# Sliding-window attention of a decoder layer: both key tiles folded into one block of 128 probabilities

## The chip, the cores and the metric

The kernel runs on one NeuronCore of a Trainium2 chip. Its engines work side by side, each on a queue of its own: TensorE (PE, with its weight loads as PEld), VectorE (DVE), ScalarE (ACT), GpSimd (POOL) and SyncE (SP, which issues most DMAs). The metric is the device time of one execution in microseconds. TensorE writes to PSUM, of which there are 8 banks of 128 x 512 float32; VectorE and ScalarE read them.

## The reference

One decoder layer for x of 1024 x 1024, float32. A norm and one projection feed two groups of heads: gated linear attention (4 heads), computed in chunks, and sliding-window attention (8 query heads, 2 key heads of 64, window 128). Then an output projection and a gated feed-forward part of width 2816 with a causal convolution of 3 taps. The change touches the sliding-window part, in which a query block of 128 rows sees its own key block and the one before:

```
i = arange(128)[:, None];  j = arange(256)[None, :]
dist = 128 + i - j
mask = (dist >= 0) & (dist < 128) & (key_abs >= 0)
s = where(mask, q k^T / 8 - slope * dist, -inf)
m = max(max(s, -1), sink)
p = exp(s - m);  p = p / (sum(p, -1) + exp(sink - m))
o = p v
```

Of the 256 keys that a row is scored against, exactly 128 lie in the window: key column c of the earlier block (j = c) where c > i, and of the own block (j = 128 + c) where c <= i. For each column c one of the two is in and the other out. The first query block has no earlier one.

## The kernel before

Rows are cut into 8 tiles t of 128. Up to some 75 us the norm and the query projection run, from then to 280 us the other projections (`dk`, `dv`, `dg`, `dr`: dense units of 24 matmuls, three for each of 8 blocks of the contraction) with both kinds of attention between them, then the output projection (`do`) and from some 370 us the feed-forward part (`fb`, `dn_P`), which no line of the change touches.

For each t, and each of two groups g of four heads, the attention steps are:

- `swa_qt(t)`: four transposes of the queries into a bank (`qpt`), split by ScalarE and VectorE into a high part `qt` and a rest `ql`.
- `swa_scores(t, g)`: eight matmuls of 256 columns put four heads' scores into two banks (`sc`). For each head VectorE adds a table `dist` (the distance, -1e30 outside the window), takes the maximum with the sink and writes the row of 256 to `pr` (line 451). Small VectorE operations make the scaled negative maximum (`sm1`). ScalarE takes the exponential of each head's 256 columns and their sum (line 457). The sums and the sink give a reciprocal (`sm2`, `sm3`, lines 459 to 462), and GpSimd multiplies all of `pr` by it (line 464).
- `swa_pt(t, g)`: for each of the two key blocks b, four transposes (`ppt`) into a bank; ScalarE copies the bank of the own block (b = 1) to `pt`, VectorE that of the earlier one (b = 0).
- `swa_pv(t)`: matmuls of the values with both halves of `pt` into a bank `pv`, which ScalarE copies out.

For t = 0 only the own block is worked on. Banks come from `bank(name)`, which takes them in turn from two pools of four. `qt`, `ql`, `pr` and `pt` are tiles of one ring of six (`k4`), smaller temporaries of a ring of four (`k2`).

The program is written as a list of events with due times (`at(s + 3.2, swa_pt, t, 0)` and so on, in units of about one dense unit), issued in the order of these times. Behind it a scheduler sets the order of each engine's queue from a model of the instructions' lengths, so that an edit moves neighbours too. The linear attention needs a mask of its own, `amask` (line 115), which `const_b` makes from an upper triangle of ones, `upper` (lines 140 to 150).

Of the kernel before, what the change touches and what calls it, by code (L numbers as in the profile page):

```python
# [9 lines left out]
F32 = mybir.dt.float32  # L10
F32R = mybir.dt.float32r
I32 = mybir.dt.int32
AF = mybir.ActivationFunctionType
ALU = mybir.AluOpType
# [3 lines left out]
P = 128  # L18
# [16 lines left out]
def hymba_layer_kernel(ctx, tc, x, mix_norm, w_in, w_alpha2, b_alpha, gla_norm,  # L35
# [3 lines left out]
    act, dve, pool, pe, sp = nc.scalar, nc.vector, nc.gpsimd, nc.tensor, nc.sync  # L39
# [15 lines left out]
    def bank(name):  # L55
        ps["n"] += 1
        if "f" in ps:
            return ps["f"][2 + ps["n"] % 2]

        for start, which in (("n2pt_6", "b"), ("do1_7", "a"), ("n2pt_3", "a")):  # L60
            if name.startswith(start):
                return ps[which].tile([P, 512], F32, tag="b", name=name)
        return ps["ab"[ps["n"] % 2]].tile([P, 512], F32, tag="b", name=name)
# [3 lines left out]
    RAW_BUFS, K4, K2, N_WARM = 3, 6, 4, 5  # L67
# [30 lines left out]
    ident = idp.tile([P, P], F32, name="ident")  # L98
# [5 lines left out]
    gl = sg.enter_context(tc.tile_pool(name="gl", bufs=1))  # L104
# [7 lines left out]
    islope = gl.tile([P, 8], F32, name="islope")  # L112
    qscale = gl.tile([P, 8], F32, name="qscale")
    tri = gl.tile([P, 2, P], F32R, name="tri")
    amask = gl.tile([P, P], I32, name="amask")
    ind = gl.tile([P, 2], F32R, name="ind")
    mhalf = idp.tile([P, 8], F32, name="mhalf")
    pool.memset(mhalf, -0.5)
# [18 lines left out]
                           fill=NEG, base=-1, channel_multiplier=-1)  # L137

    def const_b():
        upper = gl.tile([P, 512], F32, tag="k2", name="upper", bufs=K2)[:, 0:P]  # L140
        pool.memset(upper, 1.0)
        pool.affine_select(out=upper, in_=upper, pattern=[[1, P]], compare_op=ALU.is_ge,
                           fill=0.0, base=0, channel_multiplier=-1)
        pool.memset(ind.bitcast(F32), 0.0)
        pool.memset(ind[0:64, 0:1].bitcast(F32), 1.0 / 16.0)
        pool.memset(ind[:, 1:2].bitcast(F32), 1.0 / 16.0)

        dve.tensor_scalar(tri[:, 0], upper, 1.0 / 16.0, ind[:, 0:1].bitcast(F32), op0=ALU.mult, op1=ALU.subtract)
        dve.tensor_scalar(tri[:, 1], upper, -1.0 / 16.0, 1.0 / 16.0, op0=ALU.mult, op1=ALU.add)
        pool.tensor_copy(amask, upper)  # L150


    xts = {}
# [119 lines left out]
    def k4_tile(name, dt=F32):  # L273
        return gl.tile([P, 1024], dt, tag="k4", name=name, bufs=K4)
# [160 lines left out]
    def swa_scores(t, g):  # L435
        q, ql = qts[t]
        s0 = P if t == 0 else 0
        pbs = []
        for j in range(4):
            if j % 2 == 0:  # L440
                pbs.append(bank(f"sc{t}_{g}_{j}").rearrange("p (j s) -> p j s", j=2))
            qc, kc = slice(j * P, (j + 1) * P), slice(t * P, t * P + 256)
            pe.matmul(pbs[-1][:, j % 2, :], lhsT=q[:, g, qc], rhs=kt[:, g, kc], start=True, stop=False)  # L443
            pe.matmul(pbs[-1][:, j % 2, :], lhsT=ql[:, g, qc], rhs=kt[:, g, kc], start=False, stop=True)
        if g == 0:
            smx[t] = [gl.tile([P, 8], F32, tag=f"sm{i}", name=f"sm{i}_{t}", bufs=2) for i in range(4)]
        mx, nm, den, es = smx[t]
        pr = k4_tile(f"pr{t}_{g}").rearrange("p (j s) -> p j s", j=4)
        for j in range(4):
            h = g * 4 + j  # L450
            dve.tensor_tensor_reduce(pr[:, j, s0:], pbs[j // 2][:, j % 2, s0:], dist[:, s0:], 1.0,
                                     sinks_s[:, h:h + 1], ALU.add, ALU.max, mx[:, h:h + 1])
        hs = slice(g * 4, g * 4 + 4)
        dve.tensor_mul(nm[:, hs], mx[:, hs], slope_n[:, hs])
        for j in range(4):
            h = g * 4 + j
            act.activation(pr[:, j, s0:], pr[:, j, s0:], AF.Exp, bias=nm[:, h:h + 1],
                           scale=2.0 ** -(h + 1), accum_out=den[:, h:h + 1])
        dve.tensor_add(es[:, hs], sinkb[:, hs], nm[:, hs])
        act.activation(es[:, hs], es[:, hs], AF.Exp)  # L460
        dve.tensor_add(den[:, hs], den[:, hs], es[:, hs])
        dve.reciprocal(den[:, hs], den[:, hs])  # L462
        n = 256 - s0
        pool.tensor_tensor(pr[:, :, s0:], pr[:, :, s0:],  # L464
                           den[:, hs].rearrange("p (j o) -> p j o", o=1).broadcast_to((P, 4, n)),
                           ALU.mult)
        pts[t, g] = pr

    def swa_pt(t, g):
        pr = pts[t, g]  # L470
        pt = k4_tile(f"pt{t}_{g}").rearrange("p (b c) -> p b c", b=2)
        for b in range(1 if t == 0 else 0, 2):
            pb = bank(f"ppt{t}_{g}_{b}")
            for j in range(4):
                pe.transpose(pb[:, j * P:(j + 1) * P], pr[:, j, b * P:(b + 1) * P], ident)  # L475
            if b:
                act.copy(pt[:, b], pb)
            else:
                dve.tensor_copy(pt[:, b], pb)
        pts[t, g] = pt  # L480

    def swa_pv(t):
# [587 lines left out]
    for c in halves:  # L1070
        split(mix_row[:, c], mix_hl[0][0:1, c], mix_hl[1][0:1, c], dve)
        pb = bank(f"mix{len(mix_ps)}")
# [25 lines left out]
    for t in range(NT):  # L1098
# [19 lines left out]
        if 4 <= t < 7:  # L1118
            at(u + SUMS, norm2_sums, t)
    at(5.3, const_a)  # L1120
    at(TV + 1.5, const_b)
    for i in range(4):
        d = 0.2 * i
# [10 lines left out]
    for t in range(NT):  # L1134
        s = 11.0 + 1.9 * t
        at(s - 0.3, swa_qt, t)
        at(s + 1.0, swa_scores, t, 0)
        at(s + 1.6, swa_scores, t, 1)
        at(s + 3.2, swa_pt, t, 0)
        at(s + 3.8, swa_pt, t, 1)  # L1140
        at(s + 4.9, swa_pv, t)
        s = TG + t
        at(s - 2.4, gla_lh, t)
        at(s - 1.4, gla_exp, t)
        at(s + 1.0, gla_tr, t)
        if t < NT - 1:
            at(s + 1.8, gla_state, t)
            at(s + 1.85, gla_mid, t + 1)
        at(s + 1.9, gla_a, t)
        at(s + 2.7, gla_o, t)  # L1150
        at(TR + t + 1.3, lambda tt=t: gate_tr(tt, psb.pop(("r", tt))))
# [37 lines left out]
    for ch, i, name in order:  # L1189
# [7 lines left out]
        if ch < 2 or (ch, i) == (2, 0):  # L1197
            n = 0
        elif ch < L - 1 or (ch, i) == (L - 1, 0):
            n = 1  # L1200
        else:
            n = 2
# [24 lines left out]
    for p in range(NPAIR):  # L1227
        for k in range(7):

            n = 7 * p + k - 2  # L1230
# [51 lines left out]
```

## Time and profile before

| what | us |
|---|---|
| median of 3 runs | 1065.81 (1065.1 to 1065.97) |
| profiled execution | 1065.66 |
| its span, first to last instruction | 1063.9 |
| TensorE busy | 1057.7 (99%) |
| VectorE busy | 788.4 (74%) |
| GpSimd busy | 629.1 (59%) |
| ScalarE busy | 495.2 (47%) |

Busy time counts an engine's instructions from start to end, and matmuls overlap, so that a full TensorE row does not say how much a matmul costs; the chain of waits, which follows the work that ended last, gives each piece the time until the next one. The granted TensorE clock is at its upper level (2.4 GHz, 1.00) in the whole span.

### The profile page before, as it was taken

How to read it: one execution, taken by the hardware profiler on the slowest of the kernel's cores; microseconds unless marked ns; L12 is line 12 of the kernel's file. 1: busy time of each engine (PE TensorE's matmuls, PEld its weight loads, DVE VectorE, ACT ScalarE, POOL GpSimd, SP SyncE). 2: the span in 40 equal slices, each digit the busy share in tenths (PEclk: the TensorE clock that was granted, in tenths of full speed). 3: DMA queues.
4: the chain of work that ended last, by engine and by line, in shares of the span. 5: the costliest groups of instructions: out<-in, count | busy, mean ns of one | idle time of the engine just before them, and what ended most of it. 6: DMA issues, size and time to landing. Idle time of an engine off the chain costs nothing.

```text
span 1063.9 us, 13937 instructions
## 1 busy us (share of the span) xinstructions
PE 1057.7 (99%) x4988; PEld 857.0 (81%) x4988; DVE 788.4 (74%) x1306; ACT 495.2 (47%) x1002; POOL 629.1 (59%) x511
## 2 busy tenths in 40 slices
PE   9999999999999999999999999999999999999998
PEld 6898878877888888788888888888888888888887
DVE  6776546564132499787989889797979898897976
ACT  5527655544340245545444444454444445444441
POOL 4582323334551104867868787877868687868750
PEclk9999999999999999999999999999999999999999
DMA  6152123102026202112111111112121111212104
GB/s 214 57 155 56 43 53 84 24 1 80 1 60 217 60 1 60 60 40 80 39 51 49 41 59 60 60 40 79 40 79 31 51 54 45 60 60 60 41 20 158
DMA packets 67502, 67.13 MB, mean 63 GB/s; under 512 B 4648, under 2 KB 52201, under 8 KB 67434
## 3 DMA queue, kind: packets, MB, share of 16 engines
q1 hardware_dynamic: 63448, 61.27, 18.7%
q10 hardware_dynamic: 3986, 4.99, 2.0%
q8 instruction: 39, 0.64, 0.3%
q14 instruction: 29, 0.24, 0.1%
HBM read 57.33 MB, written 4.19 MB: 58 GB/s over the span
## 4 chain that ended last, share of the span: by engine, by line
PE 99%; DMA 1%; POOL 0%; SPq 0%; ACT 0%; DVE 0%; issue 0%
PE fb L815 39%; PE dn_P L996 18%; PE do L318 8%; PE dg L318 4%; PE dr L318 4%; PE dv L318 4%; PE dq L318 3%; PE dk L318 2%; PE gb L815 2%; PE dq L688 2%; PE pv L487 2%; PE ppt L475 1%; PE dl L1025 1%; PE fb L1025 1%; PE sc L443 1%; PE go L582 1%
## 5 line engine op out<-in xcount | busy, mean ns | idle before, releaser
L1000 DVE TENSOR_TENSOR acc<-acc,dn_P 128x1024 f32<-128x1024 f32 x140 | 169.8, 1214 | 65.3 <-PE dn_P L996 65.1
L996 PE MATMUL dn_P<-dw,dg 128*128 128x512 f32 x840 | 215.8, 393 | 0.0
L996 PEld LDWEIGHTS dn_P<-dw,dg 128*128 128x128 f32 x840 | 157.7, 188 | 37.1
L318 PE MATMUL do<-wow,big 128*128 128x512 f32 x384 | 92.9, 398 | 0.0
L95 POOL TENSOR_TENSOR dw<-dn,dw 128x512 fp32r<-128x512 f32 x50 | 69.5, 1390 | 25.4 <-PE dn_P L996 22.3
L318 PEld LDWEIGHTS do<-wow,big 128*128 128x128 f32 x384 | 71.1, 188 | 16.3
L867 ACT COPY ca<-fb 128x512 f32<-128x512 f32 x62 | 36.4, 587 | 72.5 <-PE fb L815 72.4
L464 POOL TENSOR_TENSOR pr<-pr,sm 128x1024 f32<-128x1024 f32 (+1 forms) x16 | 28.6, 1789 | 65.4 <-DVE sm L462 40.1
L815 PE MATMUL fb<-big,A11w 128*128 128x512 f32 x252 | 63.0, 396 | 0.0
L815 PE MATMUL fb<-big,S4w 128*128 128x512 f32 x252 | 62.9, 396 | 0.0
L815 PE MATMUL fb<-big,S1w 128*128 128x512 f32 x252 | 62.9, 396 | 0.0
L815 PE MATMUL fb<-ex,S2w 128*128 128x512 f32 x252 | 62.8, 397 | 0.0
L815 PE MATMUL fb<-ex,S3w 128*128 128x512 f32 x252 | 62.8, 396 | 0.0
L822 DVE SCALAR_TENSOR_TENSOR ua<-fb,cc,ua 128x511 f32<-128x511 f32 x84 | 62.2, 740 | 0.5 <-ACT ua L827 0.3
L815 PE MATMUL fb<-big,A12w 128*128 128x512 f32 x252 | 62.5, 396 | 0.0
L815 PE MATMUL fb<-ex,A22w 128*128 128x512 f32 x252 | 62.5, 397 | 0.0
L815 PEld LDWEIGHTS fb<-big,S1w 128*128 128x128 f32 x252 | 47.4, 188 | 11.6
L815 PEld LDWEIGHTS fb<-big,A11w 128*128 128x128 f32 x252 | 47.4, 188 | 11.6
L815 PEld LDWEIGHTS fb<-big,S4w 128*128 128x128 f32 x252 | 47.4, 188 | 11.6
L815 PEld LDWEIGHTS fb<-ex,S2w 128*128 128x128 f32 x252 | 47.4, 188 | 11.4
L815 PEld LDWEIGHTS fb<-ex,A22w 128*128 128x128 f32 x252 | 47.4, 188 | 11.4
L815 PEld LDWEIGHTS fb<-ex,S3w 128*128 128x128 f32 x252 | 47.4, 188 | 11.4
(430 smaller groups left out, 2450.6 us busy)
## 6 DMA issues: line engine op xcount, KB each, us to landing
up<-in_w_up_dram SPq DMA_DIRECT2D x44, 512.0 KB, 3.8
dn<-in_w_down_dram SPq DMA_DIRECT2D x22, 512.0 KB, 3.5
acc<-in_x_dram SPq DMA_DIRECT2D x8, 512.0 KB, 7.5
out_dram<-acc SPq DMA_DIRECT2D x15, 256.0 KB, 2.0
xt<-in_x_dram SPq DMA_DIRECT2D x7, 512.0 KB, 4.5
vraw<-in_w_in_dram SPq DMA_DIRECT2D x4, 512.0 KB, 3.8
graw<-in_w_in_dram SPq DMA_DIRECT2D x4, 512.0 KB, 3.7
qt<-qt ACTq DMA_DIRECT2D x16, 128.0 KB, 2.2
```

What stands on the lines that cost most here:

```text
L95: (eng or pool).tensor_sub(lo, src, hi.bitcast(F32))
L318: pe.matmul(pb[:, :n], lhsT=big[:, t, k, ra, :], rhs=ws[k][:, rb, :n], start=(k == 0 and i == 0), stop=(k == KD - 1 and i == 2))
L443: pe.matmul(pbs[-1][:, j % 2, :], lhsT=q[:, g, qc], rhs=kt[:, g, kc], start=True, stop=False)
L464: pool.tensor_tensor(pr[:, :, s0:], pr[:, :, s0:], den[:, hs].rearrange("p (j o) -> p j o", o=1).broadcast_to((P, 4, n)), ALU.mult)
L487: pe.matmul(pb[g * 64:(g + 1) * 64, :], lhsT=vv[:, t - 1 + b, g * 64:(g + 1) * 64], rhs=pts[t, g][:, b, :], start=(b == b0), stop=(b == 1))
L688: pe.matmul(pb, lhsT=big[:, t, k, ra, :], rhs=blocks["q"][k][:, rb, :], start=(k == 0 and i == 0), stop=(k == KD - 1 and i == 2))
L815: pe.matmul(pb, lhsT=w[:, ra, k, :], rhs=b_operand(bn, k, rb), start=(onto is None and i == 0), stop=(i == 11), skip_group_check=onto is n ...
L822: dve.scalar_tensor_tensor(dst, src, w, dst, op0=ALU.mult, op1=ALU.add)
L867: act.copy(dst, pb)
L996: pe.matmul(pb[:, i], lhsT=g[:, ra, c:c + P], rhs=w[:, rb, :], start=(onto is None and n == 0), stop=(n == 2), skip_group_check=onto is no ...
L1000: dve.tensor_add(acc, acc, pb)
L1025: pe.matmul(pb[:, c0:c1], lhsT=g[:, ra, (t % 4) * P:(t % 4 + 1) * P], rhs=w[:, rb, c0:c1], start=(ch == NCH - 2 and i == 0), stop=(ch == N ...
```

## The change

After the four score steps of a pair (t, g) with t > 0, VectorE takes the maximum of the two halves of `pr`; the result has 128 columns per head. Exponential, sum, normalisation and transposes work on those alone, one bank of transposes instead of two. Behind the transposes VectorE multiplies the bank by the triangle `upper` (keys of the own block) into the second half of `pt`, and subtracts that from the bank into the first half (keys of the earlier block). For t = 0 ScalarE copies the bank as before. The score matmuls, the score steps and `pv` keep their shapes. `upper` becomes a tile of its own that lives as long as `amask` did, and `amask` is the same bytes read as integers.

```diff
@@ -112,7 +112,8 @@
     islope = gl.tile([P, 8], F32, name="islope")
     qscale = gl.tile([P, 8], F32, name="qscale")
     tri = gl.tile([P, 2, P], F32R, name="tri")
-    amask = gl.tile([P, P], I32, name="amask")
+    upper = gl.tile([P, P], F32, name="upper")
+    amask = upper.bitcast(I32)
     ind = gl.tile([P, 2], F32R, name="ind")
     mhalf = idp.tile([P, 8], F32, name="mhalf")
     pool.memset(mhalf, -0.5)
@@ -137,7 +138,6 @@
                            fill=NEG, base=-1, channel_multiplier=-1)
 
     def const_b():
-        upper = gl.tile([P, 512], F32, tag="k2", name="upper", bufs=K2)[:, 0:P]
         pool.memset(upper, 1.0)
         pool.affine_select(out=upper, in_=upper, pattern=[[1, P]], compare_op=ALU.is_ge,
                            fill=0.0, base=0, channel_multiplier=-1)
@@ -147,7 +147,6 @@
 
         dve.tensor_scalar(tri[:, 0], upper, 1.0 / 16.0, ind[:, 0:1].bitcast(F32), op0=ALU.mult, op1=ALU.subtract)
         dve.tensor_scalar(tri[:, 1], upper, -1.0 / 16.0, 1.0 / 16.0, op0=ALU.mult, op1=ALU.add)
-        pool.tensor_copy(amask, upper)
 
 
     xts = {}
@@ -452,31 +451,34 @@
                                      sinks_s[:, h:h + 1], ALU.add, ALU.max, mx[:, h:h + 1])
         hs = slice(g * 4, g * 4 + 4)
         dve.tensor_mul(nm[:, hs], mx[:, hs], slope_n[:, hs])
+
+        if t:
+            dve.tensor_tensor(pr[:, :, P:], pr[:, :, 0:P], pr[:, :, P:], ALU.max)
+        pr = pr[:, :, P:]
         for j in range(4):
             h = g * 4 + j
-            act.activation(pr[:, j, s0:], pr[:, j, s0:], AF.Exp, bias=nm[:, h:h + 1],
+            act.activation(pr[:, j], pr[:, j], AF.Exp, bias=nm[:, h:h + 1],
                            scale=2.0 ** -(h + 1), accum_out=den[:, h:h + 1])
         dve.tensor_add(es[:, hs], sinkb[:, hs], nm[:, hs])
         act.activation(es[:, hs], es[:, hs], AF.Exp)
         dve.tensor_add(den[:, hs], den[:, hs], es[:, hs])
         dve.reciprocal(den[:, hs], den[:, hs])
-        n = 256 - s0
-        pool.tensor_tensor(pr[:, :, s0:], pr[:, :, s0:],
-                           den[:, hs].rearrange("p (j o) -> p j o", o=1).broadcast_to((P, 4, n)),
+        pool.tensor_tensor(pr, pr, den[:, hs].rearrange("p (j o) -> p j o", o=1).broadcast_to((P, 4, P)),
                            ALU.mult)
         pts[t, g] = pr
 
     def swa_pt(t, g):
         pr = pts[t, g]
         pt = k4_tile(f"pt{t}_{g}").rearrange("p (b c) -> p b c", b=2)
-        for b in range(1 if t == 0 else 0, 2):
-            pb = bank(f"ppt{t}_{g}_{b}")
-            for j in range(4):
-                pe.transpose(pb[:, j * P:(j + 1) * P], pr[:, j, b * P:(b + 1) * P], ident)
-            if b:
-                act.copy(pt[:, b], pb)
-            else:
-                dve.tensor_copy(pt[:, b], pb)
+        pb = bank(f"ppt{t}_{g}")
+        for j in range(4):
+            pe.transpose(pb[:, j * P:(j + 1) * P], pr[:, j], ident)
+        if t == 0:
+            act.copy(pt[:, 1], pb)
+        else:
+            own = upper.rearrange("p (q c) -> p q c", q=1).broadcast_to((P, 4, P))
+            dve.tensor_mul(pt[:, 1].rearrange("p (j c) -> p j c", j=4), pb.rearrange("p (j c) -> p j c", j=4), own)
+            dve.tensor_sub(pt[:, 0], pb, pt[:, 1])
         pts[t, g] = pt
 
     def swa_pv(t):
```

TensorE's queue behind the `pv` of t = 1, before (`ppt2_0_0` and `ppt2_0_1` are the transposes of t = 2, g = 0 for the two key blocks, `sc3_1` the scores of t = 3, g = 1):

```order
L487 MATMUL pv1_1729<-pt1_0_1582,vv_128 64x512
L487 MATMUL pv1_1729<-pt1_1_1635,vv_128 64x512
L475 MATMUL ppt2_0_0_1736<-ident_72,pr2_0_1563 128x128 x4
L475 MATMUL ppt2_0_1_1742<-ident_72,pr2_0_1563 128x128 x4
L443 MATMUL sc3_1_0_1748<-kt_127,qt3_1600 128x256
L444 MATMUL sc3_1_0_1748<-kt_127,ql3_1601 128x256
L443 MATMUL sc3_1_0_1748<-kt_127,qt3_1600 128x256
```

The same place in the changed kernel:

```order
L489 MATMUL pv1_1722<-pt1_0_1583,vv_128 64x512
L489 MATMUL pv1_1722<-pt1_1_1632,vv_128 64x512
L475 MATMUL ppt2_0_1729<-ident_72,pr2_0_1563 128x128 x4
L442 MATMUL sc3_1_0_1736<-kt_127,qt3_1596 128x256
L443 MATMUL sc3_1_0_1736<-kt_127,ql3_1597 128x256
L442 MATMUL sc3_1_0_1736<-kt_127,qt3_1596 128x256
L443 MATMUL sc3_1_0_1736<-kt_127,ql3_1597 128x256
```

One of the two rows of four transposes is gone; what stands before and behind it is the same.

VectorE's queue before, from the last score steps of t = 3, g = 1 to the copy of the transposes of t = 2, g = 1 and what follows (`sm` are the small sums, `ql4` a part of the queries of t = 4):

```order
L451 ISA pr3_1_1758,sm0_3_1684<-sc3_1_2_1753,dist_87,sinks_s_131 128x256
L451 ISA sm0_3_1684 128x1
L451 ISA pr3_1_1758,sm0_3_1684<-sc3_1_2_1753,dist_87,sinks_s_131 128x256
L451 ISA sm0_3_1684 128x1
L431 TENSOR_TENSOR ql4_1779<-qpt4_1773,qt4_1778 64x512
L479 COPY pt2_1_1791<-ppt2_1_0_1792 128x512
L459 TENSOR_TENSOR sm3_3_1687<-sinkb_130,sm1_3_1685 128x4
L454 TENSOR_TENSOR sm1_3_1685<-sm0_3_1684,slope_n_88 128x4
L459 TENSOR_TENSOR sm3_3_1687<-sinkb_130,sm1_3_1685 128x4
```

The same place in the changed kernel (`pr3_0<-pr3_0` is the maximum of the two halves, `pt2_1<-ppt2_1,upper` the product, `pt2_1<-ppt2_1,pt2_1` the difference):

```order
L450 ISA pr3_1_1746,sm0_3_1676<-sc3_1_2_1741,dist_87,sinks_s_131 128x256
L450 ISA sm0_3_1676 128x1
L453 TENSOR_TENSOR sm1_3_1677<-sm0_3_1676,slope_n_88 128x4
L456 TENSOR_TENSOR pr3_0_1680<-pr3_0_1680 128x4x128
L481 TENSOR_TENSOR pt2_0_1728<-ppt2_0_1729,pt2_0_1728 128x512
L430 TENSOR_TENSOR ql4_1768<-qpt4_1762,qt4_1767 64x512
L480 TENSOR_TENSOR pt2_1_1780<-ppt2_1_1781,upper_92 128x512
L453 TENSOR_TENSOR sm1_3_1677<-sm0_3_1676,slope_n_88 128x4
L456 TENSOR_TENSOR pr3_1_1746<-pr3_1_1746 128x4x128
L462 TENSOR_TENSOR sm3_3_1679<-sinkb_130,sm1_3_1677 128x4
L481 TENSOR_TENSOR pt2_1_1780<-ppt2_1_1781,pt2_1_1780 128x512
L462 TENSOR_TENSOR sm3_3_1679<-sinkb_130,sm1_3_1677 128x4
```

Between the last score step and the second half of `pt2_1` stood `ql4` and one copy; now two maxima, two differences and a product stand there with `ql4`, and the difference of g = 0 comes behind four score steps and a maximum.

## Rows read from the trace of the kernel before

**Rows 1.** Page, busy time by engine and the chain that ended last, whole span.
```profile
PE 1057.7 (99%) x4988; PEld 857.0 (81%) x4988; DVE 788.4 (74%) x1306; ACT 495.2 (47%) x1002; POOL 629.1 (59%) x511
...
PE 99%; DMA 1%; POOL 0%; SPq 0%; ACT 0%; DVE 0%; issue 0%
```

**Rows 2.** Windows, 75 to 280 us: length, busy us (instructions) by engine, clock, DMA.
```profile
75.00:280.00 205.00, 205.00 (x1207) 166.94 (x1205) 112.25 (x359) 117.82 (x349) 74.32 (x71) 1.00 0.19 48
```

**Rows 3.** Lines on PE, 75 to 280 us: instruction, count, busy us, mean ns, idle.
```profile
L475 PE MATMUL ppt<-ident,pr 128*128 128x128 f32 x120 | 16.1, 275 | 0.0
```

**Rows 4.** Line 475, whole span: count, duration ns least/middle/most, first and last start.
```profile
L475 PE MATMUL ppt<-ident,pr x120: 270/273/329, 104.9 to 256.1; 128*128 128x128 f32 x120
```

**Rows 5.** Chain, pieces in order of time, 75 to 280 us: start, length, what.
```profile
105.05 0.44 PE ppt L475 x4
...
136.84 1.87 PE pv L487 x8
138.70 1.02 PE ppt L475 x8
...
140.55 0.12 PE sc L444
140.68 0.44 PE qpt L424 x4
141.11 0.87 PE ppt L475 x8
141.99 5.60 PE dv L318 x24
147.59 0.48 PE bd L513 x4
148.06 0.34 PE dec L523 x4
```

**Rows 6.** Lines on DVE by form, 80 to 280 us.
```profile
L451 DVE CUSTOM_DVE_ANT_0 pr<-sc,dist,sinks_s 128x256 f32<-128x256 f32 x56 | 23.9, 478 | 20.1 <-PE pv L487 18.7 <-PE sc L444 1.4
L431 DVE TENSOR_TENSOR ql<-qpt,qt 64x512 fp32r<-64x512 f32 x15 | 10.3, 690 | 4.6 <-ACT qt L429 4.4
L479 DVE COPY pt<-ppt 128x512 f32<-128x512 f32 x14 | 9.6, 686 | 4.6 <-PE ppt L475 4.6
...
L451 DVE DVE_READ_ACCUMULATOR2_ANT sm<- 128x1 f32 x64 | 5.2, 82 | 0.0
...
L459 DVE TENSOR_TENSOR sm<-sinkb,sm 128x4 f32<-128x4 f32 x16 | 3.7, 229 | 0.3
...
L454 DVE TENSOR_TENSOR sm<-sm,slope_n 128x4 f32<-128x4 f32 x16 | 2.5, 156 | 0.2
```

**Rows 7.** Line 95 on DVE, 80 to 280 us: duration ns least/middle/most.
```profile
L95 DVE TENSOR_TENSOR gw<-graw,gw x4: 679/924/1778, 154.1 to 160.5; 128x512 fp32r<-128x512 f32 x4
L95 DVE TENSOR_TENSOR rw<-rraw,rw x4: 692/738/994, 250.9 to 256.5; 128x512 fp32r<-128x512 f32 x4
```

**Rows 8.** Lines on ACT by form, 80 to 280 us.
```profile
L457 ACT ACTIVATE pr<-pr,sm 128x256 f32<-128x256 f32 x56 | 27.8, 498 | 6.7 <-DVE sm L454 3.7 <-DVE sm L459 3.0
...
L477 ACT COPY pt<-ppt 128x512 f32<-128x512 f32 x16 | 9.4, 586 | 2.7 <-PE ppt L475 2.6
...
L457 ACT ACTIVATE pr<-pr,sm 128x128 f32<-128x128 f32 x8 | 3.1, 390 | 0.0
```

**Rows 9.** Lines on POOL by form, 80 to 280 us.
```profile
L464 POOL TENSOR_TENSOR pr<-pr,sm 128x1024 f32<-128x1024 f32 x14 | 26.5, 1896 | 65.4 <-DVE sm L462 40.1 <-issue 8.6 <-ACT gsq L588 7.2
...
L464 POOL TENSOR_TENSOR pr<-pr,sm 128x512 f32<-128x512 f32 x2 | 2.1, 1038 | 0.0
```

**Rows 10.** Waits, 75 to 280 us: who waited for whom, us in total, times, longest.
```profile
POOL pr L464 <- DVE sm L462: 40.1, 8, 13.8
...
DVE pr L451 <- PE pv L487: 18.7, 6, 7.9
...
DVE pt L479 <- PE ppt L475: 4.6, 3, 2.2
```

## The prediction

> **What bounds the kernel now.** I read the page first, then the one stretch in which attention runs, then single lines of it. The page shows TensorE busy 99% of the span, and a chain of waits that is TensorE for 99% [rows 1]; no other engine passes 74%. A busy TensorE can hide pauses, so the stretch itself has to be looked at: from 75 to 280 us, where every instruction that the change touches lies, TensorE is busy 205.00 of 205.00 us at full granted clock, VectorE 112.25, ScalarE 117.82, GpSimd 74.32 [rows 2]. The waits of that stretch belong to the others, and they wait for TensorE or for each other: VectorE's score step waits 18.7 us for `pv`, GpSimd's normalisation 40.1 us for VectorE's small sums [rows 10]. So the stretch lasts as long as TensorE's queue takes to run through. What shortens that queue shortens the kernel, and what is added elsewhere is free until TensorE has to wait for it.
>
> **TensorE: 56 transposes fewer.** Before, one tile and group (t, g) has 8 transposes of probabilities (4 for t = 0): 7 x 2 x 8 + 2 x 4 = 120, as the trace counts [rows 3, 4]. Afterwards each has 4, that is 64. The order shows it: two rows of four between `pv1` and `sc3_1` become one, and the neighbours stay. What is one worth? Its busy time, 275 ns [rows 3], is a pipeline's length and not what the queue pays. The chain gives that: 8 in 0.87 us, 4 in 0.44 us [rows 5], so 0.109 us each. 56 x 0.109 = 6.1 us. Eight of them behind a `pv` take 1.02 us [rows 5]; if the removed four were always the slower half (1.02 - 0.44 = 0.58), 14 x 0.58 = 8.1 us. I take 6.1, since the extra 0.15 belongs to what follows `pv` and stays with the four that remain.
>
> The Trainium skill (TensorE: Matmul & The Clock Gate, Part 4: PE-mode transpose) gives about 275 ns for such a transpose in one kernel's context. The duration here agrees, 273 ns in the middle [rows 4]; taken as the price, the change would be worth 56 x 0.275 = 15.4 us. The chain speaks against that with 0.44 us for four.
>
> **VectorE: more work, under cover.** For each of the 14 pairs (t, g) with t > 0 the copy of one transposed half (0.686 us [rows 6]) goes, and three operations come: the maximum, the product with the mask, the difference. Product and difference read PSUM and one SBUF operand over 512 columns; the nearest row, `ql` less `qpt` at the same width, takes 0.690 us [rows 6]. The maximum reads two SBUF operands and no row has it. The nearest are differences of two SBUF operands: `gw` 0.679 to 1.778 us, `rw` 0.692 to 0.994, with middles of 0.924 and 0.738 [rows 7]. I take 0.8, near `rw`, since GpSimd has less to do here than while `gw` is made. Sum: 14 x (0.8 + 0.69 + 0.69 - 0.69) = +20.9 us; with the maximum at 0.68 or 1.78 it is +19 or +35. Mean load in the stretch goes from 112 of 205 to 133 of 199 us, 67%: no bound on average.
>
> The spread of `gw` is where VectorE runs beside GpSimd. The Trainium skill (GPSIMD Engine Reference, Specifications) says that GpSimd shares its SBUF interfaces with VectorE and that instructions with two SBUF inputs contend. The 0.679 to 1.778 us of `gw` [rows 7] fit this; it would put the maximum at the upper end.
>
> Locally the cover is thinner, so I counted one burst in the new order, behind `ppt2_0`. VectorE runs product 0.69, four score steps with their reads 4 x (0.478 + 0.082) = 2.24, `sm1` 0.16, maximum 0.8, difference 0.69, half of `ql4` 0.69, product 0.69, `sm1` 0.16, maximum 0.8, `sm3` 0.23, difference 0.69 [rows 6]: 7.8 us until the second half of `pt2` is there. TensorE, which needs it for the second matmul of `pv2`, has until then eight score matmuls 0.96, `qpt` 0.44, `ppt2_1` 0.44, a dense unit 5.60, `bd` 0.48, `dec` 0.34, four score matmuls 0.48 and one `pv` (an eighth of 1.87, 0.23): 9.0 us [rows 5]. The margin is 1.2 us. The other tiles have a dense unit of 5.6 us between their last transposes and `pv` as well. So I put this wait at 0. If both maxima took 1.78 us, the 2.0 us more would leave TensorE waiting 0.8 us there. Behind the late difference stand `sm3`, the other half of `ql4` and the small sums that GpSimd's normalisation waits for; the bank of the transposes is also held until the difference has read it, some 4.6 us where a copy gave it back after 0.7.
>
> **ScalarE and GpSimd: less work, worth nothing by itself.** 56 exponentials shrink from 256 to 128 columns, 0.498 to 0.390 us each, and 14 copies of 0.586 us go: -6.0 - 8.2 = -14.2 us [rows 8]. The 14 products of `pr` with the reciprocals shrink from 1.896 to 1.038 us: -12.0 us [rows 9]. Neither engine sets the end, so no term. They do shorten the chain from scores to `pv`: per pair +0.8 (maximum), -0.43 (four exponentials), -0.86 (normalisation), -0.44 (transposes), +0.69 (a second operation behind them), -0.2 us in all. The mask conversion on GpSimd and the tile that `upper` held in a ring happen once. Fewer banks are taken, 14 in all, an even number, so that the alternation of the two bank pools comes out as before where the later stages begin; TensorE's order there is unchanged.
>
> **Sum.** The profiled execution took 1065.66 us, span 1063.9, the remaining 1.76 around it untouched. 1065.66 - 6.1 = 1059.6 us. The median before is 1065.81, 0.15 higher, within the spread of its runs (1065.1 to 1065.97). Bounds for the likeliest case: 1058.5 (a few of the groups give 0.58) to 1061.0 (a wait of about 0.1 us per pair, 14 of them).
>
> **Rivals.**
> - The removed transposes are worth more: 14 x 0.58 = 8.1 us, 1057.5 us. For it: the 1.02 us behind `pv`. Against: other groups of eight take 0.87, and the start-up stays with the first four.
> - A transpose is worth its duration: 1050.3 us. Against it stands the chain. Only if TensorE's queue paid the 273 ns.
> - VectorE comes late in some bursts: it decides from a maximum of about 1.4 us, where the margin of 1.2 is used up by two of them. With 0.8 us at four bursts the saving falls to 2.9 and the time is 1062.8. For it: 1.78 us occurs in `gw`. Against: in `rw` the longest is 0.99.
> - The time of the stretch is set not by TensorE's queue but by the loop from `pv` over scores, softmax and transposes to the next `pv` (VectorE waits 18.7 us for `pv` [rows 10]). That loop runs once per t and shortens by only 0.2 us, 7 x 0.2 = 1.4 us, 1064.3. Against: TensorE would show idle time, and it has none [rows 2]. The change not doing what it says is not a case of its own: the order has the 64 transposes.
> - Slower: the product stands at the head of VectorE's queue until its transposes are done, and the score steps behind it, which free the score banks, stand too. The old copy waited at this place 4.6 us in 3 cases, 1.5 each [rows 10]. If each of the 14 products stood 1.5 us, with the difference's 0.69 on top and the margin of 1.2 gone, TensorE would wait 1.0 us at each: 14.0 - 6.1 = +7.9, 1073.6 us. The change turns slower from 6.1 / 14 = 0.44 us per pair. Against: only 3 of 14 waited before.
>
> **How the numbers follow.** Likeliest case 70%, transposes worth more 8%, worth their duration 1%, VectorE late in some bursts 11%, bound by the loop or all of the saving eaten 6%, slower 4%. A measurement of this kernel can tell about 0.2% (2.1 us) from no change, so that faster means below 1063.7: 70 + 8 + 1 + 11 = 90%; same 6%, slower 4%. The range takes in the likeliest case, the 8.1 us saving and the near half of the late bursts: 1057.4 to 1062.7.
>
> **What would show it.** Right: 64 transposes, still 0.44 us for four in the chain, TensorE without idle time in a stretch that ends some 6 us earlier, and the same 6 us at the end, VectorE near 133 us busy in it, GpSimd 12 and ScalarE 14 us less. Wrong: waits of TensorE for `pt`, for a score bank or for `ql`, a maximum above 1.4 us, or a dense unit that starts later than its predecessor's end allows; and if the 6 us are there at 270 us but not at the end, a load or a later stage sets the time.

## The result, and the profile of the changed kernel

The changed kernel takes 1060.07 us (median of 4 runs, 1058.27 to 1060.29), against 1065.8 before (4 runs, 1065.1 to 1065.97): a ratio of 0.9944, interval 0.9927 to 0.9961, faster by 5.7 us. 1059.6 was forecast. The profiled execution took 1060.03 us, 5.63 less than that of before. One run of an experiment below (late triangle and warm-up, 1140.88 us at a mean granted clock of 0.851) was a slow one and is left out of its median. Where the 5.63 us lie can be read from three marks in the two traces: the first matmul of `dk` (attention follows), the first of `do` (attention is over) and the end of the span.

| | before | changed | difference |
|---|---|---|---|
| start of the span to `dk` | 61.10 | 62.55 | +1.45 |
| `dk` to `do` | 252.88 | 245.80 | -7.08 |
| `do` to the end | 749.96 | 749.96 | 0.00 |

So there are two results: attention gives back more than the 6.1 us forecast, and the start, which was to stay as it was, loses 1.45 us.

**Attention.** The page, in two lines (busy time by engine, then the chain that ended last), answers to [rows 1]; the window (length, then busy us and instructions by engine, granted clock, DMA share, GB/s) answers to [rows 2], with the end 5.6 us earlier:

```profile
PE 1051.5 (99%) x4932; PEld 851.7 (80%) x4932; DVE 799.3 (76%) x1334; ACT 482.7 (46%) x988; POOL 617.8 (58%) x510
...
PE 98%; DMA 0%; issue 0%; DVE 0%; POOL 0%; SPq 0%; ACT 0%; POOLq 0%
```

```profile
75.00:274.40 199.40, 199.26 (x1163) 162.05 (x1162) 123.57 (x389) 105.71 (x337) 63.70 (x69) 1.00 0.19 51
```

TensorE is busy 199.26 of the 199.40 us and the bound is the same. There are 64 transposes with the old duration (line 475, the view of [rows 4]):

```profile
L475 PE MATMUL ppt<-ident,pr x64: 270/272/329, 106.3 to 250.4; 128*128 128x128 f32 x64
```

The chain's pieces answer to [rows 5], at the same place, behind the `pv` of t = 1:

```profile
137.43 1.87 PE pv L489 x8
139.30 0.59 PE ppt L475 x4
...
141.27 0.44 PE ppt L475 x4
```

Four transposes behind a `pv` take 0.59, where eight took 1.02: the 0.15 at the head of the block stays, as the prediction had it, and 0.43 goes. Added over all transposes, from each start to the next instruction's, attention saves 6.35 us in them (12.75 to 6.40). Where does the rest of the 7.08 come from? In the same sum `pv` gets 1.0 us shorter, 16.08 to 15.08, though not one of its matmuls changed. In the chain before, the `pv` of t = 5 came in two pieces with scores between. Each of its four matmuls is two entries of the chain; the first matmul alone took 1.00, the other three 1.86:

```profile
215.89 1.00 PE pv L487 x2
216.90 0.32 PE sc L443
...
217.57 1.86 PE pv L487 x6
```

In the changed kernel the same `pv` is one block, 2.86 less 1.87:

```profile
213.22 1.87 PE pv L489 x8
```

Nobody wrote that: the scheduler put the block together when it planned the new program. In a block the matmuls of the two groups g start in pairs, 6 to 8 ns apart, so that four take the time of two pairs; a matmul left alone takes as long as a pair. (The `pv` of t = 2 is split after its first matmul in both kernels.) The other groups of instructions add up to +0.27, of which `dec` +0.46, `dg` +0.24, `go` -0.20 and `dv` -0.10 are the largest: other neighbours in the queue, and in `dec` one wait, shown below. The profiled execution then adds up: -6.35 - 1.00 + 0.27 + 1.45 = -5.63 us.

**VectorE** by lines, the view of [rows 6]:

```profile
L450 DVE CUSTOM_DVE_ANT_0 pr<-sc,dist,sinks_s 128x256 f32<-128x256 f32 x56 | 23.7, 477 | 16.2 <-PE pv L489 14.8 <-PE sc L443 1.4
...
L481 DVE TENSOR_TENSOR pt<-ppt,pt 128x512 f32<-128x512 f32 x14 | 9.6, 684 | 0.2
L456 DVE TENSOR_TENSOR pr<-pr 128x512 f32<-128x512 f32 x14 | 9.6, 683 | 0.0
L480 DVE TENSOR_TENSOR pt<-ppt,upper 128x512 f32<-128x512 f32 x14 | 9.6, 683 | 3.7 <-PE ppt L475 3.7
```

The maximum takes 0.683 us, not 0.8, and none of the 14 took longer than 0.693. Its waits, and those of the neighbours, against [rows 10]:

```profile
POOL pr L466 <- DVE sm L465: 24.6, 7, 8.3
...
DVE pr L450 <- PE pv L489: 14.8, 6, 5.5
ACT pr L460 <- DVE pr L456: 13.5, 7, 2.6
...
DVE pt L480 <- PE ppt L475: 3.7, 3, 1.6
```

ScalarE now waits 13.5 us for the maximum, a wait that did not exist before. TensorE's own waits of 0.15 us or more in the whole span are these four, none of them in attention:

```profile
PE warm L1068 <- DVE warm L124: 1.7, 1, 1.7
PE mix L1076 <- DVE mix L95: 0.7, 1, 0.7
PE dq L690 <- POOL qw L295: 0.5, 1, 0.5
PE gb L817 <- ACT big L255: 0.2, 1, 0.2
```

One shorter wait is new: the 0.14 us by which the window falls short of 199.40. The chain, which before stays on TensorE through all of attention, leaves it here for VectorE's queue and comes back at `cs`, a matmul of the linear attention:

```profile
203.14 0.02 DVE sm L450
...
203.21 0.66 PE cs L557 x8
```

So at this one place VectorE is no longer under cover, by 0.14 us.

The burst that was counted out behind `ppt2_0` can be read off. VectorE's timeline (start, length, what), with the first product and the difference that ends the burst:

```profile
140.95 0.69 DVE L480 TENSOR_TENSOR pt<-ppt,upper 128x512 f32<-128x512 f32 x1
...
146.40 0.68 DVE L481 TENSOR_TENSOR pt<-ppt,pt 128x512 f32<-128x512 f32 x1
```

and TensorE's, with the first matmul of `pv2` and the three others:

```profile
148.40 1.07 PE L489 MATMUL pv<-pt,vv 128*64 128x512 f32 x2
...
150.30 1.93 PE L489 MATMUL pv<-pt,vv 128*64 128x512 f32 x6
```

From the end of `ppt2_0` in the chain (139.89, above) to the end of that difference (147.08) are 7.2 us, where 7.8 was counted, and to the second matmul of `pv2`, the first that needs the difference, 10.4, where 9.0 was counted. The margin is 3.2 us and was forecast at 1.2; even the first matmul, which needs only the earlier difference of g = 0, begins 1.3 us behind this one. The order inside is another than I had: score steps still run when the transposes are done, the product has to wait for them, and six score matmuls stand between the first matmul of `pv2` and the second. Between the other tiles' difference and `pv` lie 2.5 to 7.3 us.

**The start.** The program begins with matmuls that only warm TensorE up (`warm`); then VectorE splits the norm's weights into a high part and a rest, which TensorE spreads over the partitions (`mix`), and the transposes of the first tile follow (`n1pt`). The second of the four waits, `mix`, was 0.3 us before and is 0.7 now. TensorE's timeline of the first 14 us, before (the wait before an instruction in brackets):

```profile
4.92 1.49 PE L1074 MATMUL mix<-mix,ones_r 128*128 128x512 f32 x3 [0.33 <-DVE mix L95]
...
6.71 0.60 PE L254 MATMUL n1pt<-ident,h 128*128 128x128 f32 x4
```

and in the changed kernel:

```profile
5.30 1.65 PE L1076 MATMUL mix<-mix,ones_r 128*128 128x512 f32 x3 [0.72 <-DVE mix L95]
...
7.61 1.05 PE L253 MATMUL n1pt<-ident,h 128*128 128x128 f32 x4
```

Two things are to be seen. The pause before `mix` is 0.39 us longer, and behind it the same four transposes take 1.05 instead of 0.60: a lower clock. The windows say 1.00 even here, but the traces' first clock record, of 2.4 GHz, begins at 9.2 us instead of 6.1. Ahead of it the matmuls of `warm` follow each other every 0.43 us, behind it every 0.23, so that the level there is the lower one, 1.2 GHz. In the kernel before, too, the upper level thus holds from 6.1 us on and not in the whole span. VectorE's timeline shows who makes TensorE wait. Before, it went to the `mix` split at once:

```profile
4.18 1.28 DVE L95 TENSOR_TENSOR mix<-mix_row,mix 1x512 fp32r<-1x512 f32 x2
```

Now it first makes the two `tri` tables, which the linear attention uses:

```profile
4.24 0.23 DVE L149 TENSOR_SCALAR tri<-upper 128x128 fp32r<-128x128 f32 x1 [0.16 <-POOL ind L146]
4.38 0.28 DVE L148 TENSOR_SCALAR tri<-upper,ind 128x128 fp32r<-128x128 f32 x1
4.58 1.27 DVE L95 TENSOR_TENSOR mix<-mix_row,mix 1x512 fp32r<-1x512 f32 x2
```

They read `upper`, and before they ran at 106 us, since `upper` had to wait its turn in the ring `k2`. As a tile of its own it is ready at 4 us, and everything that reads it moves to the front.

### The profile page after: what moved, and what is told of

Read it like the earlier page. It is cut to its first block, busy times and chain, and to the rows that moved or that the text cites. A ratio compares the mean times of both kernels' runs of the same rounds, so it can differ in the third digit from the quotient of the medians.

```text
span 1058.3 us, 13835 instructions
## 1 busy us (share of the span) xinstructions
PE 1051.5 (99%) x4932; PEld 851.7 (80%) x4932; DVE 799.3 (76%) x1334; ACT 482.7 (46%) x988; POOL 617.8 (58%) x510
## 4 chain that ended last, share of the span: by engine, by line
PE 98%; DMA 0%; issue 0%; DVE 0%; POOL 0%; SPq 0%; ACT 0%; POOLq 0%
PE fb L817 39%; PE dn_P L998 18%; PE do L317 8%; PE dg L317 4%; PE dr L317 4%; PE dv L317 4%; PE dq L317 3%; PE dk L317 2%; PE gb L817 2%; PE dq L690 2%; PE pv L489 1%; PE dl L1027 1%; PE fb L1027 1%; PE sc L442 1%; PE go L584 1%; PE ga L575 1%
## 5 line engine op out<-in xcount | busy, mean ns | idle before, releaser
L817 PE MATMUL fb<-ex,S2w 128*128 128x512 f32 x252 | 62.8, 397 | 0.0
L817 PE MATMUL fb<-ex,S3w 128*128 128x512 f32 x252 | 62.8, 396 | 0.0
L817 PEld LDWEIGHTS fb<-big,A12w 128*128 128x128 f32 x252 | 47.3, 188 | 11.1
```

The source lines that it names most:

```text
L817: pe.matmul(pb, lhsT=w[:, ra, k, :], rhs=b_operand(bn, k, rb), start=(onto is None and i == 0), stop=(i == 11), skip_group_check=onto is n ...
```

## The experiments

All were run beside the kernel before on the same chips, with medians of 1065.48, 1065.46 and 1065.39 us (15 runs in each of the three sets). The ratios are over all runs and differ a little from the quotients of the medians. The theory: attention gains some 7 us, and 1.2 to 1.5 are lost at the start because `upper` became a tile of its own. Rivals: the start differs by chance from run to run; the lateness of the start, not the clock, costs the time; the transposes are worth less than 6.1 and VectorE's load eats some of it; the gain is one of a luckier order.

**The changed kernel again.**

> The changed kernel as it is, beside the others on the same chip. Theory A: 1060.0 us in nearly all runs. Rival R: a mixture of about 1058.3 and 1060.1 us.

Measured: 1060.02 us (1058.3, 1060.18, 1060.36, 1058.33, 1060.02), ratio 0.9941 (0.9929 to 0.9954). With the first four runs, six of nine lie near 1060.2 and three at 1058.3, nothing between. The profiled execution was one of the latter:

```profile
5.29 1.10 PE L1076 MATMUL mix<-mix,ones_r 128*128 128x512 f32 x3 [0.70 <-DVE mix L95]
...
6.70 0.60 PE L253 MATMUL n1pt<-ident,h 128*128 128x128 f32 x4
```

The pause is there, 0.70, but the transposes run at the full pace at 6.70, and `dk` begins at 60.89. Attention takes 245.80 as before. So the pause does not by itself cost the 1.45 us; the clock does, which after this pause comes up early in some executions and late in most. The Trainium skill (TensorE: Matmul & The Clock Gate, Part 1: The HAM clock gate) says that how many matmuls run at the lower level at a kernel's start varies from run to run; these two traces of one kernel agree, 1.05 and 0.60 us for the same four transposes.

**The triangle made at its old place.**

```diff
     def const_b():
-        pool.memset(upper, 1.0)
-        pool.affine_select(out=upper, in_=upper, ...
+        u0 = gl.tile([P, 512], F32, tag="k2", name="u0", bufs=K2)[:, 0:P]
+        pool.memset(u0, 1.0)
+        pool.affine_select(out=u0, in_=u0, ...
...
+        pool.tensor_copy(upper, u0)
```

> The changed kernel with one edit: the triangle is made in a ring tile at its old place, as before the change, and copied into the lasting tile; the attention steps are untouched, and nothing stands in front of the norm's small products on VectorE at the start any more. Theory A (the changed kernel saves some 7 us between 80 and 270 us, and loses 1.45 us in its first 12 us because two operations on the triangle stand on VectorE's queue ahead of the split of the norm weights): the first unit dq is back at its old time, TensorE idles about 0.33 us instead of 0.72 in front of the second mix matmul, time 1058.6 us, between 1058.0 and 1059.2. Rival R (the lost 1.45 us at the start is chance of when TensorE's clock rises, and the order there does not matter): 1060.0 us in most runs, 1058.3 in some, as for the changed kernel.

Measured: 1058.79 us (1057.9 to 1059.32), ratio 0.9933 (0.9921 to 0.9946). Attention 245.77, `dk` at 60.48; the pause is back at its old length and the clock is up:

```profile
4.92 1.10 PE L1078 MATMUL mix<-mix,ones_r 128*128 128x512 f32 x3 [0.33 <-DVE mix L95]
...
6.33 0.60 PE L255 MATMUL n1pt<-ident,h 128*128 128x128 f32 x4
```

No run lies near 1060.2. The edit of `upper` is what costs the changed kernel 1.2 us in the median.

**The edit of `upper` alone, in the kernel before.**

```diff
-    amask = gl.tile([P, P], I32, name="amask")
+    upper = gl.tile([P, P], F32, name="upper")
+    amask = upper.bitcast(I32)
...
-        upper = gl.tile([P, 512], F32, tag="k2", name="upper", bufs=K2)[:, 0:P]
...
-        pool.tensor_copy(amask, upper)
```

> The kernel before with one edit: the triangle gets a lasting tile of its own and serves as the mask of the linear attention as well; the sliding-window attention is as before. VectorE's two operations on the triangle move to the start, as in the changed kernel. Theory A: 1.4 us slower than before, 1067.2 us, between 1066.7 and 1067.7. Rival R: 1065.8 us, as before.

Measured: 1067.33 us (11 runs; nine from 1067.0 to 1067.8, two at 1065.5), ratio 1.0012 (1.0003 to 1.0021). Attention 252.89, as before; `dk` at 62.83 instead of 61.10. The loss is there without the change in attention, 1.85 us between the medians, and again the times stand in two groups. In this trace the clock rises at 10.3 us.

```profile
7.60 1.06 PE L253 MATMUL n1pt<-ident,h 128*128 128x128 f32 x4
```

**The changed kernel with two more warm-up matmuls**, that fill the pause and leave the `mix` split as late as it is.

```diff
-    RAW_BUFS, K4, K2, N_WARM = 3, 6, 4, 5
+    RAW_BUFS, K4, K2, N_WARM = 3, 6, 4, 7
```

> The changed kernel with seven warm-up matmuls in front instead of five, which fill TensorE's pause before the second mix matmul; VectorE's order stays. If the loss at the start is one of TensorE's clock (its pause of 0.72 us lets the clock rise later, 9.2 us into the span instead of 6.1): clock up earlier, transposes of the first tile at 0.60 us for four instead of 1.05 and 0.77, time near 1058.9 us. If the loss is VectorE's lateness by itself (0.4 us) and what follows from it: 1060.0 us or more, since two matmuls of 0.23 to 0.43 us are added.

Measured: 1058.76 us (1058.36 to 1059.33), ratio 0.9935 (0.9923 to 0.9948).

```profile
1.66 3.35 PE L1068 MATMUL warm<-warm,ones_r 128*128 128x512 f32 x7 [1.66 <-DVE warm L124]
4.81 1.59 PE L1076 MATMUL mix<-mix,ones_r 128*128 128x512 f32 x4
...
6.71 0.60 PE L253 MATMUL n1pt<-ident,h 128*128 128x128 f32 x4
```

The pause is gone, the transposes take 0.60, and the time is that of the kernel with the late triangle, with `tri` still ahead of `mix`. So the lateness of the split is not what costs the time. What does is the lower clock that follows TensorE's pause of 0.7 us in most executions. (Two more matmuls also add work; the late triangle, which adds none, gives the same time.)

**The transposes of t > 0 issued twice** (with the late triangle, into the same bank), so that their number is 120 again and nothing else is undone.

```diff
-        for j in range(4):
+        for j in range(4 if t == 0 else 8):
+            j %= 4
             pe.transpose(pb[:, j * P:(j + 1) * P], pr[:, j], ident)
```

> The changed kernel with the late mask, and for t > 0 the four transposes of each pair issued twice into the same bank: 56 transposes more on TensorE, nothing else added. If a transpose costs TensorE's queue 0.109 us, 56 x 0.109 = 6.1 us more than the version with the late mask (1058.8): 1064.9 us, and the attention (first dk to first do matmul) 251.9 us instead of 245.8; the remaining 1.0 us of the 7.1 that the changed kernel saves there then belongs to the new order of pv and the score matmuls, not to the transposes. Rival, the whole saving is the transposes: 7.1 us more, 1065.9. Rival, a transpose costs its duration of 0.272: 15 us more, 1074. Rival, the saving comes from banks and softmax work and not from TensorE's queue: under 3 us more.

Measured: 1064.36 us (1063.64 to 1064.85, 11 runs), ratio 0.999 (0.9981 to 0.9998), 5.6 us over the same kernel with each once. In the trace the transposes' sum rises by 6.35 us, 6.40 to 12.74, and attention by 5.85 to 251.62; `dec` gives back 0.39, the wait of 0.14 included. 56 transposes at 0.113 us: the main term by itself. The 1.1 us that are left to the kernel before agree with the 1.0 of the `pv` that is no longer split.

**The maximum two and four times** (late triangle).

```diff
-            dve.tensor_tensor(pr[:, :, P:], pr[:, :, 0:P], pr[:, :, P:], ALU.max)
+            for _ in range(2):
+                dve.tensor_tensor(pr[:, :, P:], pr[:, :, 0:P], pr[:, :, P:], ALU.max)
```

> The changed kernel with the late mask, the maximum of each pair taken twice: 14 operations of 0.683 us, 9.6 us more on VectorE. If VectorE's work lies under TensorE's queue, as the prediction has it: no change, 1058.8 us within 0.5, TensorE without waits. Rival (VectorE's lateness already decides in some bursts): 14 x 0.68 less what is left of the margin, 3 us or more added.

Measured: 1060.26 us (1059.74 to 1060.46), ratio 0.9951 (0.9937 to 0.9965), 1.5 us more where no change was expected. I first took that for VectorE's load, which is 133.82 us of 205 here. But TensorE idles 0.10 us of 205 in this trace, less than the 0.14 without the second maximum. In the sums attention is 1.2 us longer, 1.0 of it in `pv`, and the chain shows the `pv` of t = 6 in two pieces with four transposes (`gt`) between, the first matmul alone:

```profile
236.14 1.00 PE pv L492 x2
237.15 0.59 PE gt L547 x4
237.73 1.86 PE pv L492 x6
```

The scheduler has planned another order. The 1.0 us is the one seen above with the other sign. The forecast of no change was missed by the order; the cover held.

> The same with the maximum four times: 28.7 us more on VectorE, which would then be busy some 153 of 199 us in the stretch, and 2.05 us more per pair, 4.1 us where two maxima stand in one burst, against a counted margin of 1.2 us at t = 2. If that margin is right, TensorE waits up to some 2 to 3 us at single bursts where no dense unit can be moved between: 1 to 8 us more, 1060 to 1067 us. If VectorE has more slack than counted: 1058.8 us.

Measured: 1060.63 us (1059.82 to 1061.07), ratio 0.9953 (0.9941 to 0.9965). VectorE is busy 152.88 of 205 us, and now TensorE does wait, for the DMA behind `ql`, which VectorE makes, and for its small sums:

```profile
PE sc L445 <- DMA ql<-ql: 0.9, 1, 0.9
...
PE gt L547 <- DVE sm L452: 0.3, 1, 0.3
...
PE dg L319 <- DVE sm L452: 0.2, 1, 0.2
```

1.4 us for 42 more maxima (of 2.1 that attention is longer). Some of them began beside a running GpSimd operation, and the longest took about what the prediction gave as its upper bound of 1.78, 1.764 us (line 459, count, duration ns least/middle/most, first and last start):

```profile
L459 DVE TENSOR_TENSOR pr<-pr x56: 671/684/1764, 105.9 to 235.6; 128x512 f32<-128x512 f32 x56
```

This trace also says something of the start. Its triangle is made late and its pause before `mix` is 0.33 us, yet the clock rises only at 7.6 us, the first transposes are partly slow, and `dk` begins at 61.57, against 60.48 with one maximum:

```profile
7.22 0.78 PE L255 MATMUL n1pt<-ident,h 128*128 128x128 f32 x4
```

Over all 13 traces `dk` begins the later, the later the clock rises, with up to 0.6 us of scatter: at 60.5 us where it rises at 4.8, at 62.8 where it rises at 10.3. So the rival of chance is right in part. The rise varies from run to run in every version, with the short pause too; what the edit of `upper` did was to make a late one likely.

**A late triangle and the warm-up together**, in search of the rest.

> The changed kernel with the late mask and seven warm-up matmuls in front instead of five. TensorE then has no pause before the small products of the norm weights, and its clock is up before the first tile in every run. Theory A: between 1058.0 and 1058.9 us, at best 0.3 us less than with the late mask alone, since little was left to lose there. If the two warm-up matmuls themselves delay the first products: 0.3 us more than the late mask alone.

Measured: 1058.49 us (four runs, 1058.08 to 1058.82), ratio 0.9934 (0.9921 to 0.9948). Either cure by itself gives the same within 0.3 us; they mend one fault.

**The four matmuls of a `pv` kept together**, by a fixed order among them, in the kernel with the late triangle, then in the kernel before, and in the former with the warm-up.

```diff
         for b in range(b0, 2):
-            for g in range(2):
+            for g in (1, 0):
...
+                        tc.add_manual_dep(ins, last[ins.engine], ...
```

> The changed kernel with the late mask, and the four matmuls of each pv kept together on TensorE, those of the second group first: the order then has none of the splits in which a single matmul of pv stands between score matmuls (the late-mask version has one, at t = 2). Nothing else is left out or added. If the 1.0 us by which the changed kernel saves more than 56 x 0.109 is one split fewer (before: t = 2 and t = 5), the last split is worth 1.0 us as well: attention from the first dk to the first do matmul 244.8 us instead of 245.8, time 1057.8 us. Rival (the first pv matmul now waits for the later half of the probabilities, and TensorE pauses): 1058.8 us or more.

Measured: 1059.28 us (1058.46 to 1060.95), ratio 0.9946 (0.9933 to 0.996): no gain. Two of the five runs (1060.40 and 1060.95) have a mean granted clock of 0.998 where the others have 1.000, for a reason that no trace shows; the profiled one took 1058.46. `pv` does fall by 1.0, 15.08 to 14.08, but the new order brings a wait for ScalarE, and attention is 245.88 as before:

```profile
PE dg L319 <- ACT vg L712: 1.3, 1, 1.3
```

Without that wait it would be 244.5, so that the 1.0 of the split is there and the wait eats it.

> The kernel before with the matmuls of each pv kept in their pairs in the same way, and nothing else. Two splits fewer: attention 250.9 us instead of 252.9, time 1063.5 us. With it and the run above, the changed kernel's transposes alone are worth 6.1 us. Rival (splits cost nothing, pv only took longer for another reason): 1065.5 us.

Measured: 1064.33 us (1064.07 to 1064.88, 11 runs), ratio 0.9989 (0.998 to 0.9998), 1.1 less than before where 1.9 was expected (1063.5). `pv` falls by 1.79, but the transposes rise by 0.99, and 0.65 of that is again a wait for ScalarE's `vg`, in the middle of eight transposes:

```profile
160.69 0.66 PE L475 MATMUL ppt<-ident,pr 128*128 128x128 f32 x4 [0.65 <-ACT vg L708]
```

Attention is 252.02; without this wait and one of 0.15 it would be 251.2, 1.7 us less than before. Here the order did not keep every `pv` whole: those of t = 4 and t = 5 stand in two halves with scores between. Yet that costs little, since each half is a pair:

```profile
168.19 1.01 PE pv L489 x4
...
170.09 1.01 PE pv L489 x4
```

Two halves take 2.02 us, 0.15 more than the block of 1.87; a split behind the first matmul takes 2.86.

> All three edits on the changed kernel: late mask, pv together, seven warm-up matmuls. If each does what it did alone: 1057.6 us, the best of all versions. If the warm-up adds nothing to the late mask: 1057.8.

Measured: 1058.66 us (1058.58 to 1060.54), ratio 0.9938 (0.9926 to 0.9951), attention 245.59, with a wait of 0.9 us for `vg`; no better than the triangle or the warm-up alone. The best versions stand together at 1058.5 to 1058.8, 1.3 us below the changed kernel; the simplest is two more warm-up matmuls.

## Why the prediction came out as it did

- **TensorE bounds the stretch, and what leaves its queue leaves the time: right.** 6.35 us of transposes went (6.1 forecast), 5.6 to 5.85 came back when they were issued again. A price of 0.275 us each is refuted, as is 0.58 for every four: the 0.15 behind `pv` stays with the four that remain.
- **VectorE under cover: right but for 0.14 us, and the size a little high.** The maximum took 0.683, not 0.8; the new waits (ScalarE's 13.5 us) do not reach TensorE; in the burst that was counted the margin is 3.2 us where 1.2 was forecast, while the one place where VectorE came late, at `cs`, was not foreseen. Its load came to 124 us of 199, not 133: [rows 6] times the counts gives 19.1 more with the maximum as measured, but 5.3 came back in other operations that had run beside GpSimd (the sums of line 461 2.3, two scalings 1.6, `gw` 1.3). Of the rest, 2.5 us is overlap: between `dk` and `do` the durations add up to 12.5 us more, the time in which VectorE is busy to 10.0, as instructions of 0.68 us start every 0.60 within a burst.
- **GpSimd and ScalarE less, no term: right.** On the page GpSimd has 11.3 us less (12.0 forecast) and ScalarE 12.5 (14.2). GpSimd's products now take 16.9 us in all, against 28.6 in [rows 9].
- **The step that failed: "The mask conversion on GpSimd and the tile that `upper` held in a ring happen once."** It was costed at nothing, by its own length. The edit took a wait away, and with it the two `tri` operations went from 106 us to 4 us, ahead of the split that TensorE waits for. That is +1.45 us in the profiled execution; in the medians undoing it gives back 1.2, filling the pause 1.3, and doing it alone costs 1.85.
- **A term that was missing: -1.0 us**, for the `pv` of t = 5, whose first matmul no longer stands alone. It nearly cancels the failed step, so that the total of 1059.6 stands 0.5 us from the measured time: that closeness is luck, and the 6.35 for 6.1 is not. The order of both kernels showed this split; I did not look for it, since I compared only the places that the change touches.
- **The rivals:** no late VectorE but for the 0.14 us, no loop from `pv` to `pv` as the bound, and no product at the head of the queue that costs anything (it waits 3.7 us in 3 cases, the copy 4.6).

What is not settled: why the clock, after the same pause, comes up late in six of nine executions (by their times; two were traced, one of each kind) and early in three, and why it once came up late without that pause.

## What to carry to other kernels

Price what leaves a full queue by the time from start to start in the chain, not by durations, and check it by putting the same instructions back. An edit that frees a resource also moves whatever waited for it: look where in the queue every reader of it now stands, at the program's start above all, where other engines' first work depends on single operations. If a scheduler plans the order, compare it over the whole stretch, since 1 us can come or go where nothing was edited: here by whether two matmuls of 64 columns stand side by side or one of them alone.

## What the runs showed of the hardware

- Four matmuls of 64 weight columns that run as one `pv` take 1.87 us, in pairs that start 6 to 8 ns apart. With other matmuls behind the first they take 1.00 and 1.86, 1.0 us more in each trace that has such a split; with scores between the two pairs they take 1.01 and 1.01, 0.15 more. A matmul alone takes as long as a pair.
- TensorE's 1.2 GHz level lasted to 5.3, 9.2 and 10.3 us in three traces with a pause of 0.7 us before `mix` (two of them of one kernel), to 4.8 to 7.6 us in seven with 0.3, and to 5.3 to 6.4 in three with none.
- VectorE operations between SBUF tiles stood, in several cases, until GpSimd's operation had ended. Before, a sum of 128x4, whose median is 0.164 us, took

```profile
129.13 1.53 DVE L461 TENSOR_TENSOR sm<-sm,sm 128x4 f32<-128x4 f32 x1 [0.60 <-ACT sm L460]
```

beside GpSimd's normalisation, and ended at 130.66, with it:

```profile
128.75 1.90 POOL L464 TENSOR_TENSOR pr<-pr,sm 128x1024 f32<-128x1024 f32 x1 [8.59 <-issue]
```

With GpSimd's normalisation halved, the 16 sums take 3.0 us instead of 5.3. The Trainium skill (GPSIMD Engine Reference, Specifications) says that GpSimd's SBUF interfaces are shared with VectorE and that instructions with two SBUF inputs contend. This agrees, and so does the 1.764 us of a maximum that began beside GpSimd's `gw`. A scaling with a single tile as input was held too, 1.57 us before and 0.14 after. The product and the difference, with one operand in PSUM, took at most 0.692 us beside GpSimd. In the changed kernel only one of the 14 maxima fell beside a GpSimd operation, which began 0.06 us after it, and it took 0.687; so the upper bound of the prediction was real, but the place of the maxima kept them from it.
